# First two weight sums of 87 of 120 seven-product pairs by adding transfers, with four pairs more, in a float32 encoder layer

## The chip, the cores and the metric

The kernel runs on one core of one Trainium2 chip. The metric is the device time of one execution in microseconds. A core has five engines that run side by side, each through its own queue of instructions: PE (TensorE, matrix products; its weight loads are listed as PEld), DVE (VectorE), ACT (ScalarE), POOL (GpSimd) and SP (SyncE, which here issues transfers). Semaphores order them. Sixteen DMA engines move data between HBM and SBUF. PE writes only into PSUM, which has eight banks.

## The reference

One layer of a bidirectional encoder on x (1, 256, 4096) in float32, with two groups of attention heads beside each other:

```python
h = rms_norm(x, g_mix)
proj = einsum('bsd,de->bse', h, w_in)        # 4096 x 11840
c_q, c_kv, k_rope, gate_a, q_b, k_b, v_b, gate_b = split(proj)
q_a = rms_norm(c_q, g_q_latent) @ w_uq       # then rotary on 64 of 192 columns
kv  = rms_norm(c_kv, g_kv_latent) @ w_ukv
y_a = mla_attention(q, k, v)                 # 16 heads, softmax over all keys
y_a = rms_norm(y_a, g_out_mla) * silu(gate_a)
y_b = dilated_mixture_attention(q_b, k_b, v_b)   # 16 heads, three dilated windows, ALiBi
y_b = rms_norm(y_b, g_out_dil) * silu(gate_b)
x = x + concat([y_a, y_b]) @ w_out           # 4096 x 4096
gate = sigmoid(rms_norm(x, g_ple) @ w_ple_gate)  # 4096 x 4096
x = x + (p @ w_ple) * gate
return rms_norm(x, g_final)
```

## The kernel before

**Products in three parts.** Every float32 operand is split into a high part `hi`, rounded to the type fp32r by ACT, and the rest `lo = src - hi`, formed by DVE (`split`). A product is then three matmuls into one PSUM bank (`mm`): high by high, low by high, high by low.

**Blocks of 1024 columns.** The wide projections are done in blocks (class `Block`): six for the dilated q, k and v (in the order q, k, v of the first eight heads, then of the other eight), one for the query latent and four for the gates (numbered n = 0 to 4), three of the output projection (k = 0 to 2; its other 1024 columns are done in chunks) and four of `w_ple_gate`. A block has 256 rows (tokens), 4096 in the contracted dimension, cut into 32 slices of 128, and two halves of 512 columns. With two token halves t and two column halves h there are four quarters of the result. A *plain step* (`plain_step`) takes one slice: it loads 128 x 1024 weights (512 KB) into a slot `raw`, splits them, and makes four products, twelve matmuls.

**Pairs with seven products.** For some slices, two at a time, the four 2 x 2 block products of the pair are made with seven products in place of eight (Winograd's form of Strassen's algorithm). `fast_steps(j)` gives four steps for pair j: product M1, then M2 and M3, then M5 and M7, then M6 and M4. They need sums of the weights and sums of the left side. The sums of the left side are made once and kept (`add_sums`, in `x_sums`, `x_sums2`, `y_sums`, `x1_sums`). The sums of the weights are made for each pair on DVE: with the two slices in `r[0]` and `r[1]`, step one (`split1`) makes T[0] from r[0] and r[1] in two operations of 128 x 512, and step two (`split2`) makes T[1] from T[0] in two more. Steps three and four split T[0] and T[1]. Products M1, M5, M6, M7 have PSUM banks of their own, added into the quarters in `d_mid`, `gate_mid`, `out_mid` or `wide_mid` once the last pair is done, while plain steps go on; the four quarters' banks are added in `d_done`, `gate_done`, `out_done` and `wide_done`.

**Order.** A string of letters gives a block's order: c is a plain step, f a step of a pair. `spread(n, lead, trail)` makes it from costs written down for the kinds of steps. The number of pairs is `FAST_QKV` (3, 7, 8, 8, 8, 7), `FAST_G` (3, 6, 7, 7, 7), `FAST_O` (6, 7, 6) and `FAST_P` (7, 7, 7, 5): 116 in all.

**Who runs ahead.** A planner (`Clock`) keeps a model of the engines' times while the program is written out, and interleaves attention tasks and other work with the steps of the blocks. The result is one fixed order for each engine. Conversions are written up to five steps ahead of the products, into a ring of pairs of tiles (three named hi and lo, and spare tiles such as B4 or B7a and B7b while nothing else uses them). Weights are loaded by SP into four slots `raw` as these become free; a pair needs two at once. POOL has little to do: it adds up squares for the attention's norms (`acc`) and issues four transfers.

**Scaling.** The dilated q, k and v are multiplied by a factor for each token (`rx`, `rxq`) in `d_mid` and `d_done`, as part of each addition. The gains of the branch norms are applied to the attention's output in `gate_rest`, as part of the product with the gate.

All instructions but the last few are issued through one helper, so the profile gives them all one line, L177; tiles tell them apart. Buffer numbers are left out there: `B<-raw,B` is a tile whose name begins with B.

Of the kernel before, what the change touches and what calls it, by code (L numbers as in the profile page):

```python
# [12 lines left out]
F32 = mybir.dt.float32  # L13
# [21 lines left out]
WARM = 6, 3  # L35

# [104 lines left out]
class Metered:  # L141
# [5 lines left out]
    def __getattr__(self, op):  # L147
        do = getattr(self.engine, op)

        def emit(out, *rest, **named):  # L150
# [11 lines left out]
            if op == "dma_start":  # L162
                us, late = (0.06 if key == "sp" else 1.0), out.shape[0] * size(out) * 4 / 400e3
                ins = []
            elif key == "pe":
# [45 lines left out]
def encoder_layer(ctx: ExitStack, tc: tile.TileContext, x, p, positions, g_mix, w_in, g_q_latent, w_uq,  # L211
# [32 lines left out]

    def split(hi, lo, src, scale=None):
# [65 lines left out]
    def rotary_tables():  # L311
        half = ROPE // 2
        w = slot("T7", [4, NT, half])
# [275 lines left out]
    def attend(h, q_src, k_src, pe, v, y, dil):  # L589
# [96 lines left out]
        nc.scalar.activation(y, by_token(o) if dil else o, AF.Copy)  # L686
# [16 lines left out]
    def head_unit(name, load, product, tags, done, n=2, time=48 * 0.119):  # L703
# [3 lines left out]
        def step(j):  # L707
            box = []

            def get():  # L710
                box.append(clock.made(wp.tile([P, 2, Q], F32, tag="raw", name=f"raw_{name}_{j}", bufs=RAW), "raw", RAW))
                load(box[0], j)
# [11 lines left out]
            new.ring, new.ring_id = HEADS_RING, "heads"  # L724
# [104 lines left out]
    def turn_steps(n, tags):  # L829
# [4 lines left out]
        def step(j):  # L834
            box = []

            def load():
                box.append(clock.made(wp.tile([P, 2, Q], F32, tag="raw", name=f"raw_r{n}_{j}", bufs=RAW), "raw", RAW))
                for k in range(2):
                    kt = 2 * j + k  # L840
                    nc.sync.dma_start(box[0][:, k].rearrange("p (h r) -> p h r", h=8),
                                      src[kt * P:(kt + 1) * P, 8 * n:8 * (n + 1), NOPE:])
# [15 lines left out]
            new.ring, new.ring_id = HEADS_RING, "heads"  # L858
# [53 lines left out]
    def gate_rest(dil, c, u):  # L912
# [6 lines left out]
        for b in range(2):  # L919
# [9 lines left out]
            for k in range(2):  # L929
                h = 4 * c + 2 * b + k  # L930
                g = G["ob" if dil else "oa"][:, h:h + 1]
                y = yb_rows(h) if dil else by_token(y_rows(ya, h))
                nc.vector.scalar_tensor_tensor(y, y, g, by_token(tp[:, k]), op0=ALU.mult, op1=ALU.mult)
# [3 lines left out]
    QUARTERS = (0, 0, "M2"), (1, 1, "X"), (0, 1, "M3"), (1, 0, "M4")  # L937

    def gate_mid(tags, blk, after=()):

        def task():
# [9 lines left out]
            for d, a, b in (((1, 1), (0, 0), "M6"), ((1, 0), (1, 1), "M5"), ((0, 1), (1, 1), "M7"),  # L951
                            ((1, 1), (0, 1), "M5")):
                nc.vector.tensor_tensor(e[d[0]][:, d[1]], e[a[0]][:, a[1]], ps[b], op=ALU.add)
# [58 lines left out]
    def d_mid(key, blk):  # L1012
        def task():
# [11 lines left out]
            yield from awaited("rx")  # L1025
            sc = [(rxq if key[0] == "q" else rx)[:, t:t + 1] for t in range(NT)]

            def add(h, t, m, old):
                nc.vector.scalar_tensor_tensor(d[h][:, t], ps[m], sc[t], old, op0=ALU.mult, op1=ALU.add)

            for t in range(NT):
                nc.scalar.activation(d[0][:, t], ps["M1"], AF.Copy, scale=sc[t])
            for t in range(NT):
                add(1, t, "M6", d[0][:, t])
            add(0, 1, "M7", d[1][:, 1])
            add(1, 0, "M5", d[1][:, 0])
            add(1, 1, "M5", d[0][:, 1])
# [4 lines left out]
    def d_done(key, blk):  # L1042
        def task():
# [3 lines left out]
            for m, t, h in quarters[2:] + quarters[:2] if key == ("v", 1) else quarters:  # L1047
                nc.vector.scalar_tensor_tensor(d[h][:, t], blk.ps[m], sc[t], d[h][:, t], op0=ALU.mult, op1=ALU.add)
# [88 lines left out]
    class Step:  # L1137

        banks, holds, ahead = (), (), False
# [4 lines left out]
        def __init__(self, load, split, run, needs=(), frees=0, time=2.73):  # L1144
            self.load, self.split, self.run, self.needs, self.frees, self.after = load, split, run, needs, frees, None
            self.hold, self.mid = 0, False
# [3 lines left out]
    Q = 512  # L1150

    class Block:
# [7 lines left out]
        NAMES = "M2", "X", "M3", "M4", "M1", "M5", "M6", "M7"  # L1160

# [10 lines left out]
        def step(self, which, *args):  # L1172
            new = Step(*args)
            new.n = self.q
# [12 lines left out]
        def load(self, kt):  # L1187
            kt = self.row(kt)
            r = clock.made(wp.tile([P, 2, self.q], F32, tag="raw", name=f"raw_{kt}", bufs=RAW), "raw", RAW)
            for lo, n in ((0, Q), (Q, Q)) if self.late and kt == 16 else ((0, 2 * self.q),):  # L1190
# [3 lines left out]
        def plain_step(self, kt):  # L1194
            box, first_ = [], self.late and kt == 16
# [17 lines left out]
            return [self.step("M2 X M3 M4", lambda: box.append(self.load(kt)), both, run, self.needs(kt), 1)]  # L1213
# [864 lines left out]
```

## Time and profile before

| | before |
|---|---|
| median of three runs | 1899.36 us (1898.67 to 1900.56) |
| span of the profiled execution | 1897.4 us |
| PE busy, matmuls | 1878.5 us, 9133 |
| DVE busy | 1696.8 us |
| ACT busy | 1140.2 us |
| POOL busy | 31.2 us |
| moved by DMA | 370.59 MB, mean 195 GB/s |

The profile was taken in an execution of its own, whose whole time is not listed among the three runs. Its span goes from the first to the last instruction; the median of the runs is 1.96 us above it. In the profile a matmul's end is modelled: a 128x512 matmul is shown with about 390 ns, and they overlap. A row of instructions gives engine, operation, written tile <- read tiles, shapes and count, then busy time and mean nanoseconds of one, then the idle time before them and what ended it.

### The profile page before, as it was taken

To read this page: it belongs to the slowest core of one execution; us is meant where nothing else is said; L and a number is where in the kernel's file an instruction comes from. 1 tells how busy PE (TensorE), PEld (TensorE's weight loads), DVE (VectorE), ACT (ScalarE), POOL (GpSimd) and SP (SyncE) were. 2 spreads that over 40 slices of the span, in tenths; PEclk is the share of its full clock that TensorE was granted. 3 is DMA by queue.
4 is the path that set the end of the run, shared out by engine and by line. 5 is a ranking of instruction groups with operands and counts; after the bars stand their busy time and mean duration, and the time that the engine had idled before them with its cause. 6 is when DMAs were issued, how large, how long until landed. Compare 5 with 4: busy or idle time off the path is not lost.

```text
span 1897.4 us, 25417 instructions
## 1 busy us (share of the span) xinstructions
PE 1878.5 (99%) x9133; PEld 1579.8 (83%) x9133; DVE 1696.8 (89%) x2354; ACT 1140.2 (60%) x1543; POOL 31.2 (2%) x41
## 2 busy tenths in 40 slices
PE   9999999999999999999999999999999999999997
PEld 7888888888899888888888999888888888888885
DVE  6999999899898989999998777999989989989897
ACT  7655656565588555556556556656655555666654
POOL 0000000000011000000000010100000000000000
PEclk9999999999999999999999999999999999999999
DMA  8666666666735566666667553576666666665665
GB/s 279 189 205 213 214 212 200 198 213 193 218 84 159 166 211 183 196 215 189 208 199 209 137 142 123 167 231 204 216 199 217 187 194 218 194 223 183 221 222 180
DMA packets 160871, 370.59 MB, mean 195 GB/s; under 512 B 29116, under 2 KB 70952, under 8 KB 160744
## 3 DMA queue, kind: packets, MB, share of 16 engines
q1 hardware_dynamic: 159896, 366.58, 62.0%
q0 software_dynamic: 512, 1.84, 0.3%
q8 instruction: 72, 1.18, 0.3%
q10 hardware_dynamic: 336, 0.54, 0.1%
q14 instruction: 55, 0.45, 0.1%
HBM read 364.72 MB, written 4.19 MB: 194 GB/s over the span
## 4 chain that ended last, share of the span: by engine, by line
PE 85%; DVE 10%; DMA 2%; issue 2%; ACT 1%; POOL 0%; DVEq 0%; ACTq 0%; POOLq 0%
PE m L177 49%; PE t L177 16%; PE s L177 11%; PE o L177 9%; DVE lo L177 3%; DVE B L177 3%; DVE T L177 2%; DVE Ah L177 1%; DMA raw<-in_w_ple_gate_dram 1%; DVE Al L177 1%; DMA raw<-in_w_in_dram 1%; ACT hi L177 0%; DVE st L177 0%; ACT B L177 0%; DVE B7b L177 0%
## 5 line engine op out<-in xcount | busy, mean ns | idle before, releaser
L177 ACT ACTIVATE hi<-raw 128x1024 fp32r<-128x1024 f32 (+2 forms) x396 | 378.9, 966 | 278.1 <-PE m L177 70.9
L177 DVE TENSOR_TENSOR lo<-raw,hi 128x1024 fp32r<-128x1024 f32 (+2 forms) x396 | 433.4, 1107 | 61.8 <-ACT hi L177 60.6
L177 PE MATMUL m<-hi,Ah 128*128 128x512 f32 (+2 forms) x659 | 247.2, 387 | 0.3 <-ACT hi L177 0.3
L177 DVE TENSOR_TENSOR B<-raw,B 128x1024 fp32r<-128x1024 f32 (+3 forms) x228 | 213.9, 947 | 20.5 <-ACT B L177 18.8
L177 PE MATMUL m<-hi,Al 128*128 128x512 f32 (+2 forms) x625 | 229.6, 380 | 0.0
L177 PE MATMUL m<-lo,Ah 128*128 128x512 f32 (+2 forms) x549 | 207.8, 379 | 1.4 <-DVE lo L177 1.3
L177 ACT ACTIVATE B<-raw 128x1024 fp32r<-128x1024 f32 (+2 forms) x142 | 135.3, 962 | 96.8 <-DMA raw<-in_w_in_dram 25.3
L177 PE MATMUL m<-hi,B 128*128 128x512 f32 (+1 forms) x524 | 179.0, 389 | 0.0
L177 PE MATMUL m<-B,Ah 128*128 128x512 f32 (+2 forms) x554 | 146.7, 359 | 0.6 <-DVE B7b L177 0.6
L177 PEld LDWEIGHTS m<-hi,Ah 128*128 128x128 f32 x659 | 124.0, 188 | 22.7 <-ACT hi L177 1.2
L177 PEld LDWEIGHTS m<-hi,Al 128*128 128x128 f32 x625 | 117.5, 188 | 21.8
L177 PEld LDWEIGHTS m<-lo,Ah 128*128 128x128 f32 x549 | 103.4, 188 | 19.9 <-DVE lo L177 2.9
L177 PEld LDWEIGHTS m<-hi,B 128*128 128x128 f32 x524 | 98.2, 188 | 19.6
L177 PEld LDWEIGHTS m<-B,Ah 128*128 128x128 f32 x554 | 95.9, 189 | 15.3 <-DVE B7b L177 1.0
L177 PE MATMUL m<-lo,B 128*128 128x512 f32 (+1 forms) x262 | 102.1, 390 | 0.1
L177 PE MATMUL m<-B,Al 128*128 128x512 f32 (+2 forms) x289 | 99.1, 371 | 0.0
L177 DVE TENSOR_TENSOR T<-raw,T 128x512 f32<-128x512 f32 (+2 forms) x110 | 85.5, 789 | 3.3 <-ACT T L177 1.7
L177 ACT ACTIVATE hi<-B 128x1024 fp32r<-128x1024 f32 x57 | 59.4, 1056 | 23.1 <-PE m L177 7.3
L177 DVE TENSOR_TENSOR lo<-B,hi 128x1024 fp32r<-128x1024 f32 x57 | 68.5, 1220 | 3.9 <-ACT hi L177 3.6
L177 PE MATMUL t<-hi,Ah 128*128 128x512 f32 x184 | 69.9, 391 | 0.0
L177 ACT ACTIVATE B<-T 128x1024 fp32r<-128x1024 f32 (+2 forms) x55 | 50.2, 916 | 22.8 <-DVE T L177 13.4
L177 PEld LDWEIGHTS m<-B,Al 128*128 128x128 f32 x289 | 54.4, 188 | 9.2
(530 smaller groups left out, 4336.9 us busy)
## 6 DMA issues: line engine op xcount, KB each, us to landing
raw<-in_w_in_dram SPq DMA_DIRECT2D x359, 512.0 KB, 4.3
raw<-in_w_out_dram SPq DMA_DIRECT2D x128, 512.0 KB, 4.6
raw<-in_w_ple_gate_dram SPq DMA_DIRECT2D x128, 512.0 KB, 4.7
raw_q<-in_w_uq_dram SPq DMA_DIRECT2D x32, 256.0 KB, 3.8
T<-in_x_dram SPq DMA_DIRECT2D x13, 512.0 KB, 6.6
raw<-in_w_in_dram SPq DMA_DIRECT2D x16, 320.0 KB, 3.1
raw_r<-in_w_uq_dram SPq DMA_DIRECT2D x16, 256.0 KB, 4.3
raw_k<-in_w_ukv_dram SPq DMA_DIRECT2D x16, 256.0 KB, 3.4
```

The lines of the kernel that those rows point to most:

```text
L177: return do(out, *rest, **named)
```

## The change

Five things are changed together.

1. In 87 pairs (all of the q/k/v blocks, all of the latent and gate blocks, and output blocks k = 0 and 1) T[0] is no longer made by DVE. A new function `ask` has POOL issue, for each such pair, two transfers that load the first and the last of the pair's four quarters into the two halves of a buffer, and then one transfer with `accum_op=ADD` that adds the second quarter, read twice, to both halves. Two buffers alternate; at most two pairs are asked for ahead of the third step that reads them. SP then loads only half of the first slice.
2. The signs are arranged so that the weight sums are additions; the subtractions move into the sums of the left side and into a common `mix` that adds up M1, M5, M6, M7.
3. q, k and v are added up unscaled, and multiplied at the end by `rx` on DVE or ACT, whichever the planner's clock has free earlier. The gains of the branch norms are applied in ACT's copy of each head's output, and `gate_rest` is one product for two heads.
4. The orders are written out as strings. Gate blocks n = 2, 3 and 4 have eight pairs instead of seven, output block k = 2 has seven instead of six: 120 pairs. The seventh and eighth sums of x, the seventh of y and the eighth of x1 are kept in parts of the left-side tiles that no product reads any more (`odd`).
5. The four raw slots become one tile with a list of free slots, so that the 33 other pairs can make both halves of T[0] in one operation when their slots lie side by side.

```diff
+ORDER_G = (
+    "cccccccccccccccfccfcfffcfcfffcfcffcccc",
+    "ccccccccccfcfcffffcffffcffffcffffcffffffcccc",
+    "ccccccfcfcfffffffcfffffcffffcfffffffcfffffffcccc",
+    "ccccccfcfcfffffffcfffffcffffcfffffffcfffffffcccc",
+    "ccccfcfcffffcffffcffffcffffcffffcffffcffffffcccc",
+)
...
+    def raw_slots(n=1):
+
+        got = raw_free[:n]
+        if n == 2:
+            got = next(([a, a + 1] for a in raw_free if a + 1 in raw_free), got)
+        for at in got:
+            raw_free.remove(at)
+        return got
...
-        nc.scalar.activation(y, by_token(o) if dil else o, AF.Copy)
+        nc.scalar.activation(y, by_token(o) if dil else o, AF.Copy, scale=G["ob" if dil else "oa"][:, h:h + 1])
...
+    def mix(e, ps):
+
+        nc.vector.tensor_tensor(e(1, 1), e(0, 0), ps["M6"], op=ALU.add)
+        nc.vector.tensor_tensor(e(1, 0), ps["M5"], e(1, 1), op=ALU.subtract)
+        nc.vector.tensor_tensor(e(0, 1), e(1, 1), ps["M7"], op=ALU.subtract)
+        nc.vector.tensor_tensor(e(1, 1), ps["M5"], e(0, 1), op=ALU.subtract)
...
-                nc.vector.scalar_tensor_tensor(d[h][:, t], blk.ps[m], sc[t], d[h][:, t], op0=ALU.mult, op1=ALU.add)
+                nc.vector.tensor_tensor(d[h][:, t], blk.ps[m], d[h][:, t], op=ALU.add)
+            yield from awaited("rx")
+            for m, t, h in quarters[2:] + quarters[:2] if key == ("v", 1) else quarters:
+                if clock.free["dve"] + 0.3 < clock.free["act"]:
+                    nc.vector.tensor_scalar(d[h][:, t], d[h][:, t], sc[t], None, op0=ALU.mult)
+                else:
+                    nc.scalar.activation(d[h][:, t], d[h][:, t], AF.Copy, scale=sc[t])
...
+    pairs, summed, asked = [], {}, [0, 0]
+
+    def ask():
+
+        while asked[0] < len(pairs) and asked[0] - asked[1] < 2 and all(f in flags for f in pairs[asked[0]][0].ready):
+            blk, j = pairs[asked[0]]
+            t, rows = blk.pre(asked[0] % 2), [slice(blk.row(k) * P, (blk.row(k) + 1) * P) for k in (2 * j, 2 * j + 1)]
+            for h in range(2):
+                nc.gpsimd.dma_start(t[:, h], blk.w[rows[h], Q * h:Q * (h + 1)])
+            nc.gpsimd.dma_start(t, blk.w[rows[0], Q:2 * Q].unsqueeze(1).to_broadcast([P, 2, Q]), accum_op=ALU.add)
+            summed[blk, j] = t
+            asked[0] += 1
...
             def split1(hi, lo):
+                at = slots[0][0]
+                if self.pre:
+                    T.append(summed.pop((self, j)))
+                    split(hi[:, 0], lo[:, 0], r[0][:, 0])
+                    return
+                T.extend(self.tmp())
+                if slots[1][0] == at + 1:
+                    plus(T[0], raw_all[:, 2 * at + 1:2 * at + 2].to_broadcast([P, 2, self.q]),
+                        raw_all[:, 2 * at:2 * at + 4:3])
                 else:
-                sub(T[0][:, 0], r[0][:, 1], r[0][:, 0])
-                sub(T[0][:, 1], r[0][:, 1], r[1][:, 1])
+                    plus(T[0][:, 0], r[0][:, 1], r[0][:, 0])
+                    plus(T[0][:, 1], r[0][:, 1], r[1][:, 1])
                 split(hi[:, 0], lo[:, 0], r[0][:, 0])
...
+            def split3(hi, lo):
+                split(hi, lo, T[0])
+                if self.pre:
+                    asked[1] += 1
...
-                    ("T5", "T6"), WP + ["B4", "B6", "B0", "B1", ("T4", "T7")])
+                    lambda: slot("T7", [2, Q]), WP + ["B4", "B6", "B0", "B1"])
+        blk.pre, blk.ready = lambda i: slot(("T5", "T6")[i], [2, Q]), ("turned g",)
...
+        blk.pre, blk.ready, blk.tmp = gate_pre, blk.fast_needs, lambda: slot("T6", [2, Q])
...
+        ask()
         while not all(f in flags for f in step.needs) or any(b in locks for b in step.banks) or i not in halves:
             advance(True)
+            ask()
             convert(lead + 1)
```

The flag "turned g" is set at step 6, once the gains that lie in T6 are turned. In the gate blocks the two buffers are the halves of B1, free once all sixteen dilated heads are done.

262 lines of the change are left out of this document (147 added, 115 removed).

## The prediction

> **What bounds the kernel now.** I read the engines' busy times on the page first, then the chain that ended last, then the windows of 100 us, and last who waited for whom on PE.
>
> ```profile
> span 1897.4 us, 25417 instructions
> PE 1878.5 (99%) x9133; PEld 1579.8 (83%) x9133; DVE 1696.8 (89%) x2354; ACT 1140.2 (60%) x1543; POOL 31.2 (2%) x41
> PE 85%; DVE 10%; DMA 2%; issue 2%; ACT 1%; POOL 0%; DVEq 0%; ACTq 0%; POOLq 0%
> ```
>
> PE is busy for 1878.5 of 1897.4 us, so 18.9 us of idle time are all that anything but fewer products could take away. The chain runs over DVE for 10%, which says that conversions often end just before their product, not that PE stood still for 190 us. The windows say where PE did stand still; their columns are the stretch, its length, busy time and instructions of PE, PEld, DVE, ACT and POOL, the clock, the DMA share and GB/s.
>
> ```profile
> 0.00:100.00 100.00, 97.42 (x449) 77.83 (x450) 83.02 (x148) 67.58 (x117) 0.74 (x7) 1.00 0.71 235
> 100.00:200.00 100.00, 99.34 (x437) 81.46 (x436) 97.20 (x127) 55.02 (x65) 0.00 (x0) 1.00 0.66 208
> 200.00:300.00 100.00, 100.00 (x443) 82.81 (x442) 95.93 (x112) 58.85 (x64) 0.00 (x0) 1.00 0.66 209
> 800.00:900.00 100.00, 100.00 (x450) 82.84 (x449) 92.78 (x113) 60.20 (x67) 0.00 (x0) 1.00 0.65 200
> 1100.00:1200.00 100.00, 99.20 (x653) 89.70 (x652) 75.40 (x132) 59.73 (x120) 12.02 (x12) 1.00 0.45 137
> 1200.00:1300.00 100.00, 99.33 (x454) 81.46 (x453) 91.59 (x134) 58.78 (x72) 1.64 (x2) 1.00 0.63 201
> 1800.00:1900.00 100.00, 83.69 (x388) 68.91 (x386) 82.85 (x126) 51.25 (x69) 0.00 (x0) 0.95 0.58 195
> PE m L177 <- DVE lo L177: 1.3, 3, 0.8
> PE m L177 <- DVE B7b L177: 0.9, 2, 0.6
> 347.35 10.88 PE m L177 x48
> ```
>
> The last stretch holds 97.4 us and is busy 83.7, so 13.7 us of the idle time are the drain at the end; the first holds 2.6. That leaves 2.6 us in the seventeen stretches between. A piece of the chain (last row: start, length, 48 products) gives the pace: 10.88/48 = 0.2267 us per 512-wide matmul. From 100 to 200 us PE ran 437 of them where the next stretch has 443: 6 x 0.2267, some 1.3 us, where the idle time shows 0.66. A busy time whose ends are modelled hides about half of each gap, so the 2.6 us stand for about 5. What PE is seen to wait for in the middle are conversions on DVE (1.3 and 0.9 us). The kernel is bound by the number of its products.
>
> **The change, part by part.** *Four pairs more.* The gate blocks n = 2, 3, 4 go from 7 to 8 seven-product pairs and the output block k = 2 from 6 to 7. Each takes one product away, three matmuls: 4 x 3 x 0.2267 = **2.7 us** less on PE. PE is full in those stretches, so this comes off the end, if the operands keep pace.
>
> *The sums off DVE.*
>
> ```profile
> L177 DVE TENSOR_TENSOR T<-raw,raw 128x512 f32<-128x512 f32 x41 | 28.0, 683 | 0.0
> L177 DVE TENSOR_TENSOR T<-raw 128x512 f32<-128x512 f32 x41 | 28.0, 683 | 0.0
> L177 DVE TENSOR_TENSOR lo<-raw,hi 128x1024 fp32r<-128x1024 f32 x309 | 374.0, 1220 | 59.4 <-ACT hi L177 58.3
> L177 DVE SCALAR_TENSOR_TENSOR B<-m,st,B 128x512 f32<-128x512 f32 x26 | 17.8, 742 | 0.1
> L177 ACT ACTIVATE B<-B,st 128x512 f32<-128x512 f32 x20 | 13.5, 708 | 0.0
> ```
>
> The two first sums cost 2 x 0.683 = 1.37 us a pair; 87 pairs lose them: 119 us. In up to 33 others two sums become one of 1024, by the lo row 1.22 for 1.37: 5 us. A pair's conversions and second sums cost DVE 0.68 + 3 x 1.22 + 2 x 0.68 = 5.7 us where two plain steps cost 2.44: the four more give some 13 back. DVE falls by about 111 us, from 89% to 84%. On the path this is worth only the waits for it. Of the roughly 5 us in the middle I take **2.2 back**, close to the 1.3 + 0.9 that the wait rows show; nothing and 5 are the ends.
>
> *q/k/v scaling, and signs.* Per q/k/v or latent block nine scaled adds of 0.742 on DVE become eight plain ones; four multiplications follow, of 0.708 if ACT takes them. ACT gains some 2 us in a block of 82; at 55 to 60% busy it has 30 us free, so I cost this at nothing. If ACT were not free, the first attention heads after the last v block would wait the 2.8 us once. The gate's products (one operation for two) and the gains moved into ACT's copy are as small and are also covered. The sign changes only swap add and subtract: nothing.
>
> *The adding transfers.* This is the added work, and before has none that adds. Per pair POOL issues two transfers of 256 KB, waits until both have landed, then issues one of 512 KB that adds; SP's first load shrinks from 512 to 256 KB. The pair now moves 1.84 MB instead of 1.05: 0.79 MB more.
>
> ```profile
> raw<-in_w_in_dram SPq DMA_DIRECT2D x359, 512.0 KB, 4.3
> T<-in_x_dram POOLq DMA_DIRECT2D x2, 512.0 KB, 5.2
> T<-in_c_dist_dram POOLq DMA_DIRECT2D x1, 512.0 KB, 4.9
> Q<-in_p_dram POOLq DMA_DIRECT2D x1, 256.0 KB, 4.9
> L177 POOL DMA_DIRECT2D T<-in_x_dram x2 | 1.5, 732 | 0.0
> 8.00:12.00 4.00, 4.00 (x21) 3.29 (x20) 1.97 (x3) 2.92 (x6) 0.00 (x0) 1.00 1.04 408
> ```
>
> Bandwidth: a block has 120 products of 3 x 0.2267 = 82 us; eight pairs add 6.3 MB, 77 GB/s on 208, so 285. The start moved 408 GB/s (last row), so there is room. If the adding transfer also occupies the engines for reading its destination, that is 0.52 MB a pair more, 51 GB/s: 336. Still under 408, with SP's loads landing later than 4.3 us.
>
> Latency: the second transfer is issued 0.73 us after the first and lands 4.9 later, then the sum lands 4.9 to 5.2 later (if adding costs nothing): 10.5 to 10.8 us from a free buffer to a finished sum. If reading the destination doubles the landing it is 5.6 + 9.8 = 15.4. I take **10.7**, near the rows. Two buffers alternate. In each, from the landing to the end of the last reader lie two sums and two conversions: 2 x 0.68 + 2 x 1.22 = 3.8 us. So a buffer turns round in 10.7 + 3.8 = 14.5 us. On PE a pair takes 4.76 us (21 matmuls) and a plain step 2.72. In the orders of gate blocks n = 2 and 3, six pairs and four plain steps lie between the third step of pair 1 and that of pair 7: 39.4 us for three turns, which need 43.5. For n = 4 a fifth plain step makes it 42.2. In the q/k/v blocks two pairs take some 16 to 17, one turn: enough.
>
> How late a sum may be is seen in a gate block (rows: start, length; first the low halves of the second and third step of a pair on DVE, then their products on PE):
>
> ```profile
> 807.11 1.22 DVE L177 TENSOR_TENSOR B7b<-raw,B7a 128x1024 fp32r<-128x1024 f32 x1
> 808.25 1.22 DVE L177 TENSOR_TENSOR lo<-B,hi 128x1024 fp32r<-128x1024 f32 x1
> 811.11 0.39 PE L177 MATMUL m<-B7a,Ah 128*128 128x512 f32 x1
> 812.47 0.39 PE L177 MATMUL o<-hi,T 128*128 128x512 f32 x1
> ```
>
> DVE ends 2.8 to 3.0 us ahead of PE; a pair's 1.37 us less on DVE makes it some 4.3. That covers the 43.5 - 39.4 = 4.1 us, barely: I cost the cycle at nothing. Behind the waiting addition on DVE stand every later conversion and the freeing of raw slots, so one that is later stops PE.
>
> The Trainium skill, page "DMA: Bandwidth & Descriptors", section "Anatomy of one DMA — SWDGE (gpsimd) path", gives a fitted 2.0 us plus bytes over 436 GB/s for a transfer issued from GpSimd. By it, as an estimate, the two steps would take 2.6 and 3.2 us and a buffer would never be late; the trace's 4.9 to 5.2 stands against it, under load, and decides. The same page, "Rules for kernel authors", says that an accumulating transfer reads its destination and writes it later; no run here shows what that adds.
>
> *At the start.* Pair 0's buffer T5 has no earlier user and POOL waits for nothing, so its two transfers go out at about 1.4 us, though the call is made at step 6: an engine runs its own queue as far as its waits let it.
>
> ```profile
> 10.24 1.06 ACT L177 ACTIVATE hi<-raw 128x1024 fp32r<-128x1024 f32 x1 [1.06 <-DMA raw<-in_w_in_dram]
> 11.33 1.23 DVE L177 TENSOR_TENSOR lo<-raw,hi 128x1024 fp32r<-128x1024 f32 x1 [1.35 <-ACT hi L177]
> 13.06 0.49 PE L177 MATMUL m<-hi,Ah 128*128 128x512 f32 x1
> ```
>
> DMA is full there. The third step's weights are converted 0.5 us before PE takes them (12.56 against 13.06). 1.05 MB at 408 GB/s are 2.6 us of transfers among the first loads. PE shows no wait there now, so the cost lies between nothing and 2.6; I take **0.5**, since the half loads share the engines with several of SP's and the later steps have more lead.
>
> Sum: -2.7 - 2.2 + 0.5 = -4.4. Span 1897.4 becomes 1893.0; the median of before is 1899.36, 2.0 above the span, so **1895.0**.
>
> **The rivals.** *Only the pairs count.* PE's idle time is small and partly not DVE's; relief brings nothing and the start costs 0.5 to 2.6: 1899.4 - 2.7 + 0.5 to 2.6 = 1897.1 to 1899.2, I say 1897.5. For it: the windows from 200 and from 800 us have no idle time with DVE at 96 and 93%. Against it: what waits there are, are for DVE. This is also the case in which the change does what it says on DVE and not on the clock.
>
> *The sum comes late.* At a latency of 12.5 us, by slower transfers or by the adding, three turns need 48.9 us. Less 39.4 and the lead of 4.3, each of the gate blocks n = 2 and 3 loses 5.2 us, n = 4 loses 2.4: 13 in all, 1895 + 13 = 1908, slower. It decides from about 11 us on; with 12 it is 8 us and the result on the line. For it: POOL's rows are 4.9 to 5.2 under lighter traffic than there will be, and no row shows an addition. Against it: those rows carry up to 512 KB in 128 to 256 pieces, the two loads only 256 KB each, so they may land sooner.
>
> *Transfers crowd out the loads.* With landing doubled (15.4) a turn takes 19 us in every one of the 13 blocks, against 15 to 17. Over three turns that is 57.6 against 39.4 to 50: some 3 to 14 us a block after the lead, 40 to 100 in all: about 1960. For it: 336 GB/s by the second count; four raw slots are all that SP can run ahead. Against it: 408 at the start.
>
> **How the numbers follow.** My case 0.52 (its own range 1891 to 1898; faster in 0.43 of it, the rest no change), only the pairs 0.20 (no change, 0.02 faster), late sums 0.21 (0.03 of it no change), crowding 0.07. About 0.2%, 3.8 us, is what a measurement of this kernel can tell from no change: faster means under 1895.6, slower over 1903.2. That gives faster 0.45, same 0.30, slower 0.25. The range is 1891 to 1911: all of the full-recovery end, and late sums to somewhat over their middle; crowding and the worst of late sums, 0.15, and 0.03 below are left out.
>
> **What would show it.** The adding transfers landing in 5 to 6 us would bear the cycle out; 7 and over would not. DVE at 83 to 85%, and PE's idle time between 100 and 1800 us under 1.5 us: my case. The same DVE with the idle time as it is: only the pairs. PE waiting for sums on DVE that wait for POOL's transfers, in the windows from 750 to 1020 us: late sums. SP's raw loads at 6 us or more and ACT waiting for them: crowding. A first product later than before, or gaps ahead of 15 us, price the start. I am wrong if PE's idle time between 100 and 1800 us grows.

## The result, and the profile after

The changed kernel takes 2089.65 us (four runs, 2084.17 to 2091.55), the kernel before 1899.26 beside it: a ratio of 1.0997, 95% interval 1.0982 to 1.1013. The forecast was 1895.0 with a range of 1891 to 1911; the change is slower by 190 us. First the page of the changed kernel: span, engines, chain.

```profile
span 2082.4 us, 25918 instructions
PE 1938.9 (93%) x9121; PEld 1600.7 (77%) x9121; DVE 1606.9 (77%) x2135; ACT 1156.5 (56%) x1575; POOL 237.1 (11%) x302
PE 39%; DMA 15%; DVE 11%; issue 4%; ACT 2%; POOL 0%; SPq 0%; DVEq 0%; ACTq 0%; POOLq 0%
```

PE issues the 12 matmuls fewer that were counted and DVE is down to 1606.9 us (expected about 1586). But PE now stands idle for 2082.4 - 1938.9 = 143.5 us where it was 18.9, and the chain runs over DMA for 15% instead of 2%. PE's busy time has grown by 60 us for fewer matmuls: some 41 are the halved clock that is taken up below; the rest I put down to the parts of the gaps that modelled matmul ends hide. The windows of 100 us, with the columns of before:

```profile
0.00:100.00 100.00, 95.00 (x431) 74.54 (x432) 79.22 (x142) 65.71 (x116) 12.70 (x22) 1.00 0.84 264
200.00:300.00 100.00, 92.20 (x396) 74.83 (x395) 69.69 (x77) 52.39 (x60) 19.01 (x24) 0.98 0.84 247
800.00:900.00 100.00, 87.83 (x366) 70.61 (x366) 74.49 (x88) 49.29 (x56) 17.66 (x23) 0.93 0.76 214
1200.00:1300.00 100.00, 99.91 (x744) 94.64 (x744) 70.14 (x119) 59.18 (x123) 7.74 (x8) 1.00 0.45 125
1700.00:1800.00 100.00, 96.96 (x425) 78.28 (x424) 84.40 (x104) 56.06 (x67) 0.00 (x0) 1.00 0.62 202
```

The loss lies where POOL has transfers: the q/k/v blocks (second row) and above all the gate blocks (third), where 366 matmuls run in 100 us instead of 450 and the clock is 0.93. In the heads (fourth) PE is full. The last row is a block of `w_ple_gate`, which has no transfer and the order of before, and yet 3 us are lost there. My own sign of being wrong is there: PE's idle time between 100 and 1800 us is 120.6 us instead of 2.6. Transfers of the same kernel (count, size, median landing):

```profile
T<-in_w_in_dram POOLq DMA_DIRECT2D x82, 256.0 KB, 6.4
T<-in_w_in_dram POOLq DMA_DIRECT2D x41, 512.0 KB, 7.8
raw_all<-in_w_in_dram SPq DMA_DIRECT2D x285, 512.0 KB, 5.0
```

And its waits (who for whom: total, times, longest):

```profile
POOL T L206 <- DMA T<-in_w_in_dram: 265.9, 41, 9.0
POOL B L206 <- DMA B<-in_w_in_dram: 201.5, 32, 8.4
ACT hi L206 <- DMA raw_all<-in_w_in_dram: 147.6, 61, 8.0
DVE T L206 <- DMA B<-in_w_in_dram: 65.0, 15, 7.4
DVE T L206 <- DMA T<-in_w_in_dram: 59.3, 21, 5.6
PE m L206 <- DVE lo L206: 36.9, 28, 5.0
```

Both rivals' marks are there, the second in part. Sums come late: the loads land after 6.4 us and the adding transfer after 7.8, not 4.9 to 5.2, and DVE waits 65.0 + 59.3 us for sums. Loads are crowded: SP's take 5.0 us instead of 4.3 (not the 6 that I had named) and ACT waits 147.6 us for them, where it waited 55.8 before. The first two rows I had counted as latency only, not as time in which POOL can do nothing else: it stands for some 6 us ahead of nearly every adding transfer, until that pair's loads have landed.

### The profile page after: what moved, and what is told of

The parts are those of the page before. It is cut to its first block, busy times and chain, and to the rows that moved or that the text cites. A ratio compares the mean times of both kernels' runs of the same rounds, so it can differ in the third digit from the quotient of the medians.

```text
span 2082.4 us, 25918 instructions
## 1 busy us (share of the span) xinstructions
PE 1938.9 (93%) x9121; PEld 1600.7 (77%) x9121; DVE 1606.9 (77%) x2135; ACT 1156.5 (56%) x1575; POOL 237.1 (11%) x302
## 4 chain that ended last, share of the span: by engine, by line
PE 39%; DMA 15%; DVE 11%; issue 4%; ACT 2%; POOL 0%; SPq 0%; DVEq 0%; ACTq 0%; POOLq 0%
PE m L206 24%; DMA B<-in_w_in_dram 7%; PE t L206 6%; PE s L206 5%; DVE lo L206 4%; PE o L206 4%; DMA raw_all<-in_w_out_dram 3%; DMA raw_all<-in_w_ple_gate_dram 2%; DVE T L206 2%; DVE Ah L206 1%; DVE B L206 1%; DMA B<-in_w_out_dram 1%; DMA raw_all<-in_w_in_dram 1%; DVE Al L206 1%; ACT hi L206 1%
## 5 line engine op out<-in xcount | busy, mean ns | idle before, releaser
L206 ACT ACTIVATE hi<-raw_all 128x1024 fp32r<-128x1024 f32 (+2 forms) x449 | 433.2, 977 | 386.2 <-DMA raw_all<-in_w_in_dram 147.6
L206 DVE TENSOR_TENSOR lo<-raw_all,hi 128x1024 fp32r<-128x1024 f32 (+2 forms) x449 | 500.7, 1126 | 133.3 <-ACT hi L206 131.9
L206 ACT ACTIVATE B<-raw_all 128x1024 fp32r<-128x1024 f32 (+2 forms) x146 | 137.1, 950 | 98.5 <-DMA raw_all<-in_w_in_dram 60.3
L206 DVE TENSOR_TENSOR B<-raw_all,B 128x1024 fp32r<-128x1024 f32 (+2 forms) x146 | 158.2, 1091 | 29.7 <-ACT B L206 29.4
L206 POOL DMA_DIRECT2D T<-in_w_in_dram x123 | 97.5, 810 | 447.3 <-DMA T<-in_w_in_dram 265.9
L206 DVE TENSOR_TENSOR T<-raw_all,T 128x512 f32<-128x512 f32 x128 | 88.5, 691 | 69.0 <-DMA T<-in_w_in_dram 59.3
L206 POOL DMA_DIRECT2D B<-in_w_in_dram x99 | 78.3, 863 | 363.8 <-DMA B<-in_w_in_dram 201.5
L206 DVE TENSOR_TENSOR T<-raw_all,B 128x512 f32<-128x512 f32 x46 | 31.7, 689 | 96.2 <-DMA B<-in_w_in_dram 65.0
L206 ACT ACTIVATE hi<-T 128x1024 fp32r<-128x1024 f32 x73 | 76.5, 1054 | 41.3 <-DVE T L206 16.5
L206 DVE TENSOR_TENSOR lo<-T,hi 128x1024 fp32r<-128x1024 f32 x73 | 88.1, 1219 | 3.6 <-ACT hi L206 3.6
```

What stands on the lines that cost most here:

```text
L206: return do(out, *rest, **named)
```

## The experiments

Theories at the start: **A**, the sums come late; **B**, the transfers crowd out the raw loads; **C**, another part of the change costs. Times are medians where there are several runs, else one run beside runs of before between 1896.8 and 1901.2 us. A single run is good to a few us only: the ten of the base lie between 1901.89 and 1905.75, the four of the last row between 1931.15 and 1941.33.

| kernel | us | runs |
|---|---|---|
| no transfers | 1940.98 | 5, ratio 1.0207 to 1.0235 |
| transfers in q/k/v only | 2006.32 | 1 |
| the same, q/k/v sums unread | 1976.60 | 1 |
| the same, three buffers | 1990.99 | 1 |
| no transfers, oldest slots | 1910.16 | 4, ratio 1.0041 to 1.0075 |
| no transfers, old orders | 1940.07 | 1 |
| no transfers, oldest slots, old orders (**the base**) | 1902.61 | 10, ratio 1.0012 to 1.0030 |
| all transfers, oldest slots | 2070.65 | 1 |
| base + q/k/v transfers | 1959.40 | 1 |
| base + q/k/v transfers, unread | 1933.95 | 1 |
| base + the same, copying | 1915.92 | 1 |
| base + q/k/v, three buffers | 1959.67 | 1 |
| base + q/k/v, three buffers from block 3 | 1931.65 | 1 |
| base + q/k/v, every second pair | 1905.42 | 1 |
| all transfers, oldest slots, old orders | 2032.74 | 1 |
| before, DVE held up in 14 places | 2010.28 | 1 |
| no transfers, four pairs with more room | 1915.01 | 5, ratio 1.0068 to 1.0095 |
| the same, gates' second pairs by transfer | 1938.90 | 4, ratio 1.0183 to 1.0220 |

**1. What do the transfers cost at all?** No block gets `pre`, so DVE makes every T[0] (edit cut; the q/k/v blocks take T5 and T6 for their sums again):

```diff
-        blk.pre, blk.ready = lambda i: slot(("T5", "T6")[i], [2, Q]), ("turned g",)
-        blk.pre, blk.ready, blk.tmp = gate_pre, blk.fast_needs, lambda: slot("T6", [2, Q])
-            blk.pre, blk.ready, blk.tmp = out_pre, [("gated", 0, c) for c in range(4)], lambda: slot("T4", [2, Q])
```

> The changed kernel without the adding transfers: all 120 pairs take their two first sums on DVE, the rest of the change stays (four pairs more, raw tiles in one buffer with slots of its own, q/k/v scaled on ACT, sums without minus signs). Theory A (the transfers' sums come late) and theory B (the transfers crowd out the raw loads) both say that the other parts cost nothing and four pairs are worth 2.7 us: 1894 to 1899 us, clock 1.00. Theory C (another part of the change costs: the slots picked for being adjacent, or the longer ACT path behind q/k/v): over 1905 us, with PE idle for some 6 us between 1600 and 2000 us from the start of the last blocks, as in the changed kernel.

1940.98 us: A and B miss, and C stands. 41.6 us of the loss are there without a single transfer. With the first of the three lines put back:

> Transfers in the six q/k/v blocks alone; the gate and output blocks take their sums on DVE again. In the changed kernel PE stands idle for 42 us between 100 and 600 us and the clock there, 0.976 in the mean, takes another 12: both theories A and B expect that loss alone to stay, so 1895 + 54 = about 1949 (1940 to 1960), with the gate and output blocks full and their clock at 1.00. If the q/k/v blocks' loss vanishes as well, the blocks act on each other and both theories fall.

2006.32: the transfers of the q/k/v blocks cost 65 us over the kernel without them; the miss against 1949 is mostly C's share.

**2. Late or crowded, with C still in it.** `unread`: DVE makes T[0] itself in T4, from raw halves that are there, while the transfers go on. `three buffers`: T4, T5 and T6 in turn from the third block on, and each adding transfer written behind the next pair's two loads. The edit of the first, cut:

```diff
                     T.append(summed.pop((self, j)))
+                    if unread(self):
+                        T[0] = slot("T4", [2, Q])
+                        plus(T[0][:, 0], r[0][:, 0], r[0][:, 0])
+                        plus(T[0][:, 1], r[1][:, 1], r[0][:, 0])
```

> As the kernel with transfers in the q/k/v blocks alone, but in q/k/v blocks 2 to 6 nobody reads what they make: DVE makes two sums of the same size in another buffer (from raw halves that are there, so these sums aren't the reference's), and the same transfers go on as fast as POOL can issue them within two pairs of the work. The DMA traffic is that of the other kernel, only the wait for the sum is gone. Theory A (late sums): the loss in the q/k/v blocks goes, 1895 to 1908 us, clock 1.00. Theory B (crowding): it stays, 1935 to 1960 us, with ACT waiting for raw loads.

> Transfers in the q/k/v blocks alone, with three buffers for the sums from the third block on, and the two loads of the next pair issued ahead of the adding transfer of this one, so that POOL waits less and a buffer may take some 24 us to turn in place of 16. Theory A: a turn of about 20 us then fits, and the loss of blocks 3 to 6 (some 36 of 54 us) goes: 1905 to 1925 us. Theory B: the bytes are the same and come closer together: 1940 to 1970 us.

1976.60 and 1990.99, or 35.6 and 50.0 over the kernel without transfers, against 65.3: outside both theories' ranges, so neither alone. C had to be cleared first.

**3. What is C?** Two candidates: the slots and the orders.

```diff
-        if n == 2:
-            got = next(([a, a + 1] for a in raw_free if a + 1 in raw_free), got)
```

> No adding transfers, and a pair takes the two raw slots that have been free longest instead of looking for two neighbours (the changed kernel takes a slot freed a moment ago where that gives neighbours). The kernel without transfers gave 1940.98 us, 41.6 over before, against both first theories. Theory C1 (the slots: loads go into slots that come free late, SP runs less far ahead): most of the loss goes, 1900 to 1910 us, and ACT waits less for raw loads in the last blocks, whose order is that of before. Theory C2 (the orders of the four blocks with one pair more are too dense for DVE, which takes the sums again): 1930 us or more.

> No adding transfers, neighbouring slots still preferred, and the four blocks back to their pairs and orders of before (four pairs fewer). C1 (slots): the loss outside those four blocks stays and most of theirs too: 1920 to 1940 us. C2 (orders): 1899 to 1905 us.

> No adding transfers, slots in the order in which they came free, and the four blocks' orders of before: what is left of the change is the scaling on ACT, the signs and the one raw tile. C1 and C2 both expect 1897 to 1901 us. A third theory, C3 (the single raw tile makes loads wait for more than their own slot, or the scaling costs): over 1905 us.

> The changed kernel as it is, with all its adding transfers, but the slots given out in the order in which they came free. With C1 the slots' part goes here as well: 2090 - 40 = 2050 us or less, and less still if the late loads and the late sums had made the same gaps longer (down to 2000). With C2 it stays at 2080 to 2095.

Without the two lines: 1940.98 to 1910.16 with the new orders, 1940.07 to 1902.61 with the old, 2089.65 to 2070.65 with all transfers. 1910.16 and 1940.07 lie at the edges of what C1 expects, 1902.61 is 1.6 us over what both give for it, and 2070.65 lies between the two. C1, the slots, is 31 to 38 us alone and 19 beside the transfers. The orders with four pairs more cost 1910.16 - 1902.61 = 7.6 us instead of giving 2.7. What remains of the change costs 3.5 (ratio 1.0021, 1.0012 to 1.0030); whether that is the scaling, the signs, the one tile, or the pair of spare tiles T4 and T7 that the q/k/v blocks' conversions lose by the change, wasn't tried apart. Neighbouring slots against oldest slots, both with the old orders and no transfers: one window of each, then one row of the waits of each.

```profile
1600.00:1700.00 100.00, 97.38 (x415) 79.44 (x414) 87.53 (x94) 58.69 (x69) 0.00 (x0) 0.97 0.62 202
```

```profile
1600.00:1700.00 100.00, 100.00 (x443) 82.67 (x442) 92.25 (x105) 61.39 (x72) 0.00 (x0) 1.00 0.65 210
```

```profile
ACT hi L206 <- DMA raw_all<-in_w_in_dram: 83.1, 41, 5.6
```

```profile
ACT hi L206 <- DMA raw_all<-in_w_in_dram: 43.4, 25, 5.1
```

The order of that block is the one of before in both. Only the choice of slots differs, and with it how often neighbours let one operation make both halves of T[0]; ACT waits twice as long for raw loads (the rows are the loads of `w_in` over the whole kernel: 83.1 us against 43.4). What follows I read from the code and have not tried by itself: with four slots, "the first two neighbours in the list of free ones" can be the slots freed last, and the load then has to wait for a conversion that has only just been written out, though an older slot lies free.

**4. The same questions on a clean base**, with oldest slots and old orders, transfers in the q/k/v blocks alone.

> From here on the base is the kernel with no transfers, slots in the order of their release and before's orders: 1902.6 us, PE full from 200 to 500 us. To it come the adding transfers in the six q/k/v blocks alone. Earlier, with neighbouring slots, they cost 2006.3 - 1941.0 = 65 us. A (late sums) and B (crowding) both expect the same again: 1955 to 1970 us.

> As the run with transfers in the q/k/v blocks alone on the base of 1902.6 us, but in q/k/v blocks 2 to 6 nobody reads what they make: DVE makes two sums of the same size in another buffer from raw halves that are there (not the reference's sums). Same transfers, no wait for them. A: what is left is the first block and little more, 1905 to 1915 us. B: raw loads still late, 1930 to 1950 us (with neighbouring slots it was 36 us over the kernel without transfers).

> Transfers in the q/k/v blocks alone on the base of 1902.6 us, three buffers from the third block on, and the next pair's two loads issued ahead of this pair's adding transfer. A: blocks 3 to 6 lose little, and about a third of the 65 us stays in the first two blocks: 1920 to 1935 us. B: 1945 to 1965 us.

`copying` takes the adding out of the third transfer of the unread run:

```diff
-            nc.gpsimd.dma_start(t, blk.w[rows[0], Q:2 * Q].unsqueeze(1).to_broadcast([P, 2, Q]), accum_op=ALU.add)
+            nc.gpsimd.dma_start(t, blk.w[rows[0], Q:2 * Q].unsqueeze(1).to_broadcast([P, 2, Q]))
```

> As the unread run on the base of 1902.6 us, but the third transfer copies in place of adding (the sums of the first block are then not the reference's; nobody reads the others). The bytes written are the same. If an adding packet holds a DMA engine twice as long as a copying one (the single packets of the changed kernel took 176 ns against 84 for 2 KB), the DMA share in the q/k/v blocks falls from about 0.93 to 0.80, the raw loads come in time and the time is 1903 to 1912 us. If it is the bytes or the number of transfers that crowd, it stays where the unread run with adding is.

The transfers cost 56.8 us; 31.3 of them stay when nobody waits for a sum; 13.3 when the third transfer only copies (1915.92, a little over the 1903 to 1912 that were expected). Both theories hold a part. Windows of the three kernels in that order:

```profile
200.00:300.00 100.00, 91.48 (x385) 73.58 (x385) 71.87 (x78) 53.55 (x59) 19.04 (x24) 0.97 0.84 241
```

```profile
200.00:300.00 100.00, 95.83 (x403) 76.95 (x403) 86.89 (x101) 54.82 (x61) 23.89 (x30) 0.97 0.94 272
```

```profile
200.00:300.00 100.00, 100.00 (x443) 82.80 (x442) 94.04 (x110) 60.30 (x67) 23.44 (x39) 1.00 0.91 312
```

The last two columns carry it: with adding, 272 GB/s already keep the DMA engines busy for 0.94 of the time, with copying 312 GB/s take 0.91. (With no reader to wait for, the unread transfers also run ahead: the last of the 41 adding transfers goes out at 466 us instead of 542, the last copying one at 399, so these two kernels load the engines more densely than the first.) The 408 GB/s of the kernel's start were no measure of the room for adding. And where PE does wait (first row), the engines aren't full, 0.84: something else sets the pace. POOL's own timeline of that kernel shows it (start, length, issues; in brackets how long POOL stood before and for whom; x2 a pair's loads, x1 its adding transfer, x3 one adding and the next loads):

```profile
208.17 1.15 POOL L206 DMA_DIRECT2D T<-in_w_in_dram  x2 [14.68 <-DVE lo L206]
214.12 2.39 POOL L206 DMA_DIRECT2D T<-in_w_in_dram  x3 [4.80 <-DMA T<-in_w_in_dram]
223.69 1.24 POOL L206 DMA_DIRECT2D T<-in_w_in_dram  x1 [7.19 <-DMA T<-in_w_in_dram]
225.59 1.14 POOL L206 DMA_DIRECT2D T<-in_w_in_dram  x2 [0.66 <-DVE B L206]
235.15 2.39 POOL L206 DMA_DIRECT2D T<-in_w_in_dram  x3 [8.42 <-DMA T<-in_w_in_dram]
...
285.81 1.24 POOL L206 DMA_DIRECT2D T<-in_w_in_dram  x1 [8.30 <-DMA T<-in_w_in_dram]
301.57 1.15 POOL L206 DMA_DIRECT2D T<-in_w_in_dram  x2 [14.52 <-DVE lo L206]
```

Eight adding transfers, from the third pair of one block to the second of the next, go out from 214.12 to 285.81: one in (285.81 - 214.12)/7 = 10.2 us. Each time POOL issues the adding transfer, then the next pair's loads, and then stands for 6 to 9 us until these have landed, since the next adding transfer in its queue waits for them. The loads land only behind the adding transfer: that of 214.12 landed at 221.41, the loads issued at 215.34 and 215.91 at 222.03 and 223.40. From the loads of one block's third pair to those of the next's, 301.57 - 208.17 = 93.4 us pass, where PE needs 82. The block ahead takes 86.8, the two behind 92.8 and 95.8: some 41 of the 57 us.

That it is this queue, and not a buffer that is read too late, the unread run shows: nobody reads there, and yet POOL's 22 adding transfers from its first row here to its last take (412.94 - 201.36)/21 = 10.1 us each.

```profile
201.36 2.39 POOL L206 DMA_DIRECT2D T<-in_w_in_dram  x3 [6.82 <-DMA T<-in_w_in_dram]
...
412.94 2.38 POOL L206 DMA_DIRECT2D T<-in_w_in_dram  x3 [6.49 <-DMA T<-in_w_in_dram]
```

**5. Is it the rate?** Three buffers once more, with the adding transfer put behind the next loads only from the third block on (the three-buffer run had delayed it in the first two blocks as well, where the buffer for those next loads is not free), then half as many transfers, then the denser orders away. The edit of the second, cut:

```diff
+            pre = self.pre if j % 2 or self.late else None
-                if self.pre:
+                if pre:
```

> As the three-buffer run, but the adding transfer is held back behind the next pair's loads only from the third block on; in the first two blocks (two buffers) it is issued at once, as in the run with plain alternation (1959.4 us). The three-buffer run gave 1959.7 with blocks 3 to 6 nearly full (idle 9.7 us from 200 to 600 against 34) and the first two worse (idle 27 us from 0 to 200 against 7.5, clock 0.85). Theory A with POOL's queue as the place (the next pair's loads stand behind the wait for this pair's): 1920 to 1935 us. If the good stretch of the later blocks was only work put off from the earlier ones: 1950 or more.

> On the base of 1902.6 us, transfers in the q/k/v blocks for every second pair only (all three pairs of the first block); DVE makes the other pairs' sums in a buffer of its own. A pair by transfer then comes every 16 us where POOL needs 10 to 12. Rate theory (A): nothing of it is late, only the start's loss stays, 1905 to 1915 us. Crowding (B), in proportion to the bytes: half of the 57 us, about 1931.

> All adding transfers, slots in the order of their release, and the four blocks back to their orders of before with a pair less (84 pairs by transfer instead of 87). Rate theory: in gate blocks 3 and 4 of the changed order six pairs come in 39.4 us, 6.6 each, where POOL needs 10.9; in the order of before a pair comes about every 8: 2070 us falls by some 30 to 45, to 2025 to 2040. If the rate does not matter: 2060 to 2070, for three transfers fewer.

1931.65, 1905.42 and 2032.74: all within what the rate theory expects, and the second, 2.8 us over the base's median and inside the spread of its ten runs, far from the proportional 1931. With every second pair, first POOL's rows, then a window of all engines:

```profile
288.84 1.14 POOL L206 DMA_DIRECT2D T<-in_w_in_dram  x2 [26.25 <-DVE B L206]
293.09 1.23 POOL L206 DMA_DIRECT2D T<-in_w_in_dram  x1 [3.10 <-DMA T<-in_w_in_dram]
371.80 1.16 POOL L206 DMA_DIRECT2D T<-in_w_in_dram  x2 [27.12 <-DVE B L206]
```

```profile
200.00:300.00 100.00, 100.00 (x443) 82.81 (x442) 86.02 (x94) 59.06 (x64) 11.87 (x15) 1.00 0.82 241
```

The blocks follow each other after 371.80 - 288.84 = 83.0 us, PE is full, and loads with no adding transfer ahead of them land after 293.09 - 288.84 = 4.2 us. The DMA engines have air at 0.82. With three buffers, POOL's rows between 300 and 400 us name no DMA any more (one of them):

```profile
313.93 2.40 POOL L206 DMA_DIRECT2D T<-in_w_in_dram  x3 [7.91 <-DVE B L206]
```

DVE's waits for sums fall from 72.8 us with two buffers to 11.9, while ACT's longest row of waits for raw loads stays, with 101.4 and 108.9 us (43.4 in the base). 29 us of loss remain, close to the 31 of the unread run: that I take for the crowding, and the other 25 to 28 for the wait. The run changes two things, a third buffer and the loads' place ahead of the adding transfer; they weren't tried apart. In the gate blocks of the run with all transfers and oldest slots the same view gives:

```profile
865.30 1.15 POOL L206 DMA_DIRECT2D B<-in_w_in_dram  x2 [25.80 <-DVE lo L206]
970.21 1.15 POOL L206 DMA_DIRECT2D B<-in_w_in_dram  x2 [27.24 <-DVE lo L206]
```

104.9 us from block to block, 23 more than PE's 82, because the order crowds the eight pairs together and POOL may be only two pairs ahead: through the block's plain steps it stands for 26 us until DVE has read a buffer. Taking the four denser orders away gives back 2070.65 - 2032.74 = 38 us, where they cost 7.6 without transfers.

**6. What does a gap cost?** The kernel before, with DVE held up in 14 places; `more` is the count in the expectation (edit cut).

```diff
+                if self.seen == 3:
+                    for _ in range(self.more):
+                        nc.vector.tensor_tensor(lo, box[0], plain(hi), op=ALU.subtract)
```

> The kernel before, without any of the change; in the third plain step of 14 blocks DVE repeats the low half's subtraction 4 to 10 times (1.22 us each, 110 us in all; the output stays the same), so that PE runs out of work for a time that grows with the count. DVE is 3 to 4.5 us ahead there, so the gaps sum to 47 to 68 us: if a gap costs only itself, 1946 to 1967 us with the clock at 1.00 outside the end. If a gap of about 2 us or more halves the granted clock for 3.41 or 6.83 us after it, as the changed kernel's records look, each costs 1.7 to 3.4 more: 1963 to 1995 us, with the clock's dips right behind the gaps and none behind the short ones.

2010.28, over both ranges. PE's idle time grows from 18.9 to 97.1 us, so the gaps were longer than foreseen; the clock shows what follows them. A gap in PE's timeline, then the windows behind it (column before the last two: granted clock):

```profile
1014.29 0.50 PE L177 MATMUL m<-B,Ah 128*128 128x512 f32 x1 [2.85 <-DVE B L177]
```

```profile
1014.00:1015.00 1.00, 0.71 (x3) 0.61 (x4) 1.00 (x2) 0.00 (x0) 0.00 (x0) 1.00 0.00 0
1015.00:1016.00 1.00, 1.00 (x6) 0.78 (x5) 1.00 (x3) 0.00 (x0) 0.00 (x0) 0.87 0.76 115
1016.00:1017.00 1.00, 1.00 (x4) 0.81 (x3) 1.00 (x2) 0.00 (x0) 0.00 (x0) 0.50 0.82 319
1017.00:1018.00 1.00, 1.00 (x4) 0.71 (x4) 0.17 (x1) 0.01 (x1) 0.00 (x0) 0.50 0.99 340
1018.00:1019.00 1.00, 1.00 (x4) 0.81 (x3) 0.00 (x0) 1.00 (x2) 0.00 (x0) 0.50 1.01 311
1019.00:1020.00 1.00, 1.00 (x6) 0.81 (x5) 0.92 (x1) 1.00 (x2) 0.00 (x0) 0.92 0.95 385
```

1.4 us after a gap of 2.85 us the clock falls to 0.50, for 0.26 + 3 + 0.16 = 3.4 us (the 0.87 and 0.92 are such shares of a us). After a gap of 1.59 us it stays (here the gap and the 10 us behind it):

```profile
919.94 0.50 PE L177 MATMUL s<-B7b,Ah 128*128 128x512 f32 x1 [1.59 <-DVE B7b L177]
```

```profile
921.00:931.00 10.00, 10.00 (x46) 8.28 (x45) 7.78 (x12) 4.11 (x7) 0.00 (x0) 1.00 0.80 255
```

In this run 13 falls of 3.4, 6.8 or 10.2 us stand behind gaps, and by the clock's records they took about 27 us of PE's work beside the 78 of the gaps. In the changed kernel there are 21 falls ahead of the end; counted in the same way they took about 41 us. That a gap costs only itself is refuted. The length of a gap alone doesn't decide: the starts of this run's 13 falls lie on one grid of 3.413 us, each behind a step of the grid in which PE shows at least 1.96 us of idle time, and no step with 1.75 or less brought one. So a gap of 2.83 us at 106 us, halved by the grid (1.39 and 1.44), left the clock alone, and one of 1.76 at 845 us, with 0.28 more in the same step, brought a fall. (In the changed kernel the border is less sharp, between 1.64 and 1.76.)

**7. Can the four pairs be had?** Orders with the pairs further apart; then every second pair of three gate blocks by transfer, into one half of B1, DVE's sums into the other.

> No transfers, slots in the order of their release, the four pairs more kept, but their orders spread over more of the block (four plain steps ahead of the first pair where the change has six, two behind the last in gate block 5 and the output block where it has four). With the change's own orders this gave 1910.2 us, PE at 97 to 98% where DVE is at 94 to 95%. If the density of DVE's work is what costs there: 1898 to 1903 us; if four more pairs can't be fed by DVE in any order: 1905 to 1911.

> As the run with more room, and every second pair of gate blocks 3 to 5 takes its first sums by transfer (12 pairs in all), DVE makes the others'. A pair by transfer comes about every 13 us in the densest part, where POOL needs 10.9: by the rate theory none is late, DVE does 1.37 us less for every second pair, and the time is at or a little under that of the run with more room, 1896 to 1901 us. If transfers cost by their bytes (57 us for 41 pairs of q/k/v, 1.4 a pair): 15 us more than the run with more room.

1915.01 and 1938.90: both miss, and the wider orders are 4.9 us slower than the change's own. Density was not what the four pairs lacked, and neither of the two sets of orders made them pay; what PE waits for there was not followed further. In the second run one buffer has to serve all transfers; POOL's loads wait 11 to 13 us for DVE to read it, so a pair takes about 18 us instead of the 13 that the order leaves. That says nothing on crowding. No version tried is faster than the kernel before.

## Why the prediction was wrong

The loss in steps, each from a pair of runs: +3.5 for scaling, signs and one tile; +7.6 for four pairs with sums on DVE; 2070.65 - 1910.16 = +160.5 for the transfers; +19.0 for the neighbouring slots: 190.6 together.

- **The turn of a buffer is the step that failed.** I took 14.5 us: 5.6 for the loads, 5.1 for the sum, 3.8 for its readers; with two buffers alternating, one pair in 7.25 us. In the busy stretches of the q/k/v run a turn took 20.2 us (mean of 26: 7.2 to the loads' landing, 0.5, 7.7 to the sum's, 4.8 until the buffer is asked for again), one pair in 10.2. My sum let one pair's loads run beside the other's adding transfer at no cost. Measured, they stand behind it in POOL's queue, land after it, and POOL waits for them. By the forecast's own numbers that queue would have kept up, with three issues of 0.73 and a landing of 4.9, 7.1 us a pair; the landing was what failed. I named what stands behind a late addition on DVE; POOL's own queue I didn't follow.
- **The latency of 10.7 us**, the larger part of that turn, was 7.2 + 0.5 + 7.7 = 15.4 there. That it equals the upper end which I worked out and didn't take is luck: I had 5.6 for the loads and 9.8 for the sum.
- **How often a pair is due** I miscounted twice. Six plain steps, not five, lie between the third steps of pairs 1 and 7 of gate block n = 4, 44.9 us; and in the full q/k/v blocks two pairs take 15.0 to 17.7 us, not 16 to 17, so that 14.5 was hardly "enough". Neither made the loss: the measured 20.2 is over all of them.
- **Bandwidth** I judged by GB/s against 408. The DMA engines' busy share showed the limit: 0.94 at 272 GB/s with adding.
- **A late PE costs more than its wait.** The halved clock behind a gap had no term in the sum: about 41 us in the changed kernel. The Trainium skill, page "TensorE: Matmul & The Clock Gate", section "What's actually happening", says that the clock halves after an idle window of about 3.4 us, and that the windows run free. The runs agree with half speed, 3.4 us and the fixed grid. They don't agree with a whole window of idle time, nor with the 3 us that its section "Why this matters for your kernels" allows: some 1.96 us within one step sufficed.
- **The slots** I took for a renaming. A line that looks for neighbours cost as much as many a mechanism, 19 to 38 us.
- **Four pairs:** the count of -2.7 was right (9121 matmuls), "if the operands keep pace" was the condition, and without transfers they don't: +7.6.
- **DVE's relief** was put at 2.2 back. With every second pair by transfer DVE does 24 us less than in the base (1665.8 against 1690.1) with no late sum, and PE's idle time is 22.0 against 21.0 us. Nothing comes back, as the rival that counted only the pairs had it.
- **The start** was put at 0.5 (nothing to 2.6): PE's idle time in the first 100 us grows from 2.3 in the base to between 3.5 and 5.7 in the runs on it or near it that issue the first block's adding transfers at once.
- **Scaling, signs and the tile**, costed at nothing: 3.5 us together with the two spare tiles, at most.
- **The rivals:** late sums and crowding were both there. The first, at 13 us, were priced for three gate blocks alone, while the pace falls short in q/k/v blocks too. The second, at 40 to 100 us, came nearest: it had a turn of 19 us in all 13 blocks, close to the measured 20.2. Against the 160.5 both lack the clock's 41, and each was priced without the other.

## What to carry to other kernels

Before a chain of load, wait and dependent transfer is moved to one engine's queue, work out its pace per item (issue, landing behind the item ahead, the wait), not only its latency, and set it against how densely the order asks for items. Buffers help only down to the queue's own pace: with one a pair took about 18 us here (gate blocks), with two 10.2 (q/k/v), and 10.1 with nobody reading. Price DMA room by the engines' busy share with the kind of transfer that is to be added, and a stall of a warm PE of some 2 us or more by its length and, by chance of where it falls, a halved clock for 3.4 us or more behind it. Picking buffers by position instead of by age cost 19 to 38 us here, so look for such rules in every "harmless" bookkeeping change.

## What the runs showed of the hardware

An adding transfer of 512 KB landed after 7.7 us in the q/k/v run and held the DMA engines longer than a copying one: exchanging it for a copy of the same size, with nobody waiting for either, took 18 us off. POOL's queue moved the same bytes in both runs; the rows give packets, MB and the share of 16 engines' span, first adding, then copying:

```profile
q0 software_dynamic: 18224, 44.83, 10.1%
```

```profile
q0 software_dynamic: 12976, 44.83, 6.7%
```

In the adding run that queue's 2-KB packets, all of them of adding transfers, took 178 ns in the median, SP's plain 2-KB packets 84; the copying run moved the same bytes in 4-KB packets of 159 ns. The Trainium skill, page "DMA: Bandwidth & Descriptors", section "Rules for kernel authors", says that an accumulating transfer reads its destination and writes it later; the longer packets agree, and are its price here. Loads issued by POOL behind an adding transfer landed after 6.7 us in the median, those with none ahead after 3.9 (issues of the run with all pairs, then of the run with every second):

```profile
T<-in_w_in_dram POOLq DMA_DIRECT2D x82, 256.0 KB, 6.7
```

```profile
T<-in_w_in_dram POOLq DMA_DIRECT2D x42, 256.0 KB, 3.9
```
